# One head, both token tiles: how the differential attention of a hybrid trunk is cut into pieces

## The chip, the cores and the metric

The kernel runs on one core of a Trainium2 chip. The metric is the device time of one execution in microseconds (us). The engines of the core are named as in the profile: PE (TensorE, matmuls; PEld its weight loads), DVE (VectorE), ACT (ScalarE), POOL (GpSimd) and SP (SyncE, which issues most of the transfers). Each engine takes its instructions in order; semaphores make one wait for another. PE writes to PSUM banks, in which a row holds 512 fp32 values.

## The reference

Two layers on 256 tokens of width 2048, all in fp32, each with attention and a short gated convolution side by side and then an MLP. Cut to what the change touches:

```python
q = _rmsnorm(q.reshape(B, S, N_HEADS, 2, HEAD_DK), q_norm_g[l])     # 8 heads, 2 maps of 64
k = _rmsnorm(k.reshape(B, S, N_HEADS, 2, HEAD_DK), k_norm_g[l])
v = v.reshape(B, S, N_HEADS, HEAD_DV)                               # 128 wide
...
s = jnp.einsum('bqhmd,bkhmd->bhmqk', qb, k).astype(jnp.float32) * scale + bias
s = jnp.where(dist >= 0, s, NEG)
p = jax.nn.softmax(s, axis=-1)
p = p[:, :, 0] - lam * p[:, :, 1]
return jnp.einsum('bhqk,bkhd->bqhd', p.astype(v.dtype), v)
...
attn = (_rmsnorm(attn, subln_g[l]) * (1.0 - lam_init)).reshape(B, S, ATTN_WIDTH)
conv = gate_b * _short_conv(gate_c * conv_in, conv_w[l])
x = x + jnp.concatenate([attn, conv.astype(attn.dtype)], axis=-1) @ w_out[l]
hm = _rmsnorm(x, mlp_norm_g[l]) @ w_up[l]
x = x + jnp.square(jax.nn.relu(hm)) @ w_down[l]
```

Each head has two maps (m = 0, 1) of 64 columns. Their softmaxes are subtracted with a weight, the difference is multiplied with the head's values, and the result is normalised per head.

## The kernel before

The 256 tokens are two tiles of 128 (t = 0, 1). Every fp32 product is made of three fp32r products: an operand is split into a high part (rounded, made on ACT) and a low part (the rest, made on DVE), and high·high, high·low and low·high are summed in PSUM (`TERMS`). Weights are streamed from memory and split in the same way, one job of 128x1024 at a time: ACT makes `whi` (L282), DVE `wlo` (L283). Three buffers hold these jobs, so the conversion of a job three ahead can begin when PE has finished a job.

A layer is `mixer` and then `mlp`. `mixer` goes through the heads in two halves of four: the projections q, k and v of a half (`linear`, L338), then the convolution's gc and ci and later gb (`linear_t`, L360), then the output projection o (L338). PE's order is the program's order; the other engines' order is set by the scheduler when the kernel is built. Everything small is a generator that is advanced between the products of a projection: `Background` keeps the pieces, and each `tick` (after six products 512 wide in `linear`, and four times per job of eight products 512 wide and eight 256 wide in `linear_t`) advances those whose time has come; `yield n` puts a piece off by n ticks. `staggered` starts several pieces some ticks apart.

- `qk_norm` (L452 to L484), started when a q or k projection is done: squares (L461), reduction, factors and the scaled tile (L469), eight ticks of rest, four transposes per token tile into one bank (L478), from which ACT makes the high part (L481) and DVE the low part (L482). In the result, `qT` or `kT`, head i has map 0 in rows 0 to 63 and map 1 in rows 64 to 127.
- `attention` (L486 to L567), started three ticks after a v projection. Half 0's runs beside the q, k and v projections of half 1; half 1's beside gc and ci. It has eight units, (t, i) for a token tile and a head, started four ticks apart. A unit makes, for each map, three products on 64 rows into a bank (L500; 128 keys wide for t = 0 and 256 for t = 1), adds the bias and takes the maximum in one DVE instruction that empties the bank (L503), then the exponentials on ACT (L510), reciprocal, factors and the combined p on DVE (L513 to L521). Nine ticks later it transposes p (L526) and splits it (L528, L529), and four ticks later multiplies it with v (L536): three products 128 wide per key tile, into a quarter of one bank (tag `av`, one buffer) that the four heads of a token tile share. After the fourth head the bank is emptied (L544), squared (L549), the factors go through POOL (L551, L382, L554), the tile is scaled (L556), and nine ticks later transposed (L562) and split into `cat` (L565, L566), which the output projection reads.

PSUM has four banks for the projections' two accumulators, three for everything named `bank` (scores, transposes) and one for `av`. The pool `bpool` holds eight tiles for qT, kT, v, the bias's raw form, `cat` and `cv`.

Of the kernel before, what the change touches and what calls it, by code (L numbers as in the profile page):

```python
# [9 lines left out]
F32 = mybir.dt.float32  # L10
# [5 lines left out]
P = 128  # L16
DEPTH = 2
# [84 lines left out]
def trunk(ctx: ExitStack, tc: tile.TileContext, x, w_in, w_out, conv_w, q_norm_g, k_norm_g,  # L102
# [8 lines left out]
    nat = ctx.enter_context(tc.tile_pool(name="nat", bufs=7))  # L111
# [29 lines left out]
    ngv = const.tile([NG, P], F32, tag="ngv", name="ngv")  # L141
# [23 lines left out]
    vec = const.tile([ROWS, P], F32, tag="vec", name="vec")  # L165
    nc.gpsimd.dma_start(vec[0:NCW, :], conv_w.rearrange("l i (k p) -> (l i k) p", p=P))
    for i, g in enumerate((q_norm_g, k_norm_g)):
        for m in range(2):
            nc.gpsimd.dma_start(
                vec[QG + i * DEPTH:QG + (i + 1) * DEPTH, m * DK:(m + 1) * DK], g)  # L170
    nc.gpsimd.dma_start(vec[QG + 2 * DEPTH:MG, :], subln_g)
    nc.gpsimd.dma_start(vec[MG:ROWS, :], mlp_norm_g.rearrange("l (k p) -> (l k) p", p=P))
    lamv = const.tile([1, 4, DEPTH, DK], F32, tag="lamv", name="lamv")
    for i, a in enumerate((lambda_q1, lambda_q2, lambda_k1, lambda_k2)):
        nc.gpsimd.dma_start(lamv[:, i], a[None])
    sel = const.tile([NB + 1, REL], F32, tag="sel", name="sel")
    nc.gpsimd.dma_start(sel, selector)
    rel = const.tile([NB + 1, 2 * NH], F32, tag="rel", name="rel")
    nc.vector.memset(rel[NB:NB + 1, :], NEG)
    nc.gpsimd.dma_start(rel[0:NB, :], rel_bias)  # L180
# [15 lines left out]
    def small_setup():  # L196
# [3 lines left out]
        by_dist = const.tile([2 * NH, REL], F32, tag="bydist", name="by_dist")  # L200
# [12 lines left out]
        prod = const.tile([1, 2, DEPTH, DK], F32, tag="lprod", name="lprod")  # L213
# [13 lines left out]
    def load_bias(l, bpool, bias):  # L227

        if l == 0:
            yield from small_setup()  # L230
# [224 lines left out]
    def qk_norm(acc, r, dst, gain, name):  # L455
# [18 lines left out]
        yield 8  # L474
        for t in range(NT):
            tp = bank(f"{name}tp{t}")
            for i in range(4):
                nc.tensor.transpose(tp[:, i * P:(i + 1) * P], out_[t][:, i * P:(i + 1) * P], ident)  # L478
            tp3 = tp.rearrange("p (h c) -> p h c", c=P)
            hi, lo = (dst[:, i, :, t * P:(t + 1) * P] for i in range(2))  # L480
            nc.scalar.activation(hi, tp3, AF.Copy, scale=gain)  # L481
            nc.vector.scalar_tensor_tensor(lo, tp3, gain, hi.bitcast(F32),  # L482
                                           op0=ALU.mult, op1=ALU.subtract)
            yield 1  # L484

    def attention(l, qT, kT, v, h0, dst, bias, tmp):  # L486

        parts = dst.open()
        avs, r0s = {}, {}

        def unit(t, i):
            W = (t + 1) * P
            h = h0 + i
            s = tmp.tile([P, 2, S], F32, tag="s", name=f"s{h}_{t}")
            mx = small.tile([P, 2], F32, tag="mx", name=f"mx{h}_{t}")
            su = small.tile([P, 2], F32, tag="su", name=f"su{h}_{t}")
            for m in range(2):
                sc = bank(f"sc{h}_{t}_{m}")
                for n, (a, b) in enumerate(TERMS):
                    nc.tensor.matmul(  # L500
                        sc[:, :W], qT[m * DK:(m + 1) * DK, a, i, t * P:(t + 1) * P],
                        kT[m * DK:(m + 1) * DK, b, i, :W], start=(n == 0), stop=(n == 2))
                nc.vector.tensor_tensor_reduce(  # L503
                    out=s[:, m, :W], in0=sc[:, :W], in1=bias[:, 2 * h + m, S - W:],
                    op0=ALU.add, op1=ALU.max, scale=1.0, scalar=-3.0e38,
                    accum_out=mx[:, m:m + 1])
            nm = small.tile([P, 2], F32, tag="nm", name=f"nm{h}_{t}")
            nc.vector.tensor_scalar_mul(nm, mx, -1.0)
            for m in range(2):
                nc.scalar.activation(s[:, m, :W], s[:, m, :W], AF.Exp, bias=nm[:, m:m + 1],  # L510
                                     accum_out=su[:, m:m + 1])
            rc = small.tile([P, 2], F32, tag="rc", name=f"rc{h}_{t}")
            nc.vector.reciprocal(rc, su)  # L513
            if i == 0:
                r0s[t] = small.tile([P, 4], F32, tag="r0", name=f"r0_{h0}_{t}")
            nc.vector.tensor_copy(r0s[t][:, i:i + 1], rc[:, 0:1])
            c = small.tile([P, 1], F32, tag="c", name=f"c{h}_{t}")
            nc.vector.scalar_tensor_tensor(c, su[:, 0:1], rc[:, 1:2], nlam[:, l:l + 1],
                                           op0=ALU.mult, op1=ALU.mult)
            p = tmp.tile([P, S], F32, tag="p", name=f"p{h}_{t}", bufs=2)  # L520
            nc.vector.scalar_tensor_tensor(p[:, :W], s[:, 1, :W], c, s[:, 0, :W],  # L521
                                           op0=ALU.mult, op1=ALU.add)
            yield 9
            tp = bank(f"ptp{h}_{t}")
            for b in range(t + 1):
                nc.tensor.transpose(tp[:, b * P:(b + 1) * P], p[:, b * P:(b + 1) * P], ident)  # L526
# [500 lines left out]
```

## Time and profile before

| | |
|---|---|
| time, median of 3 runs | 2181.18 us (2179.99 to 2181.38) |
| the profiled execution: its own time, its span | 2181.14 us, 2179.4 us |
| granted TensorE clock | 0.999 |
| busy: PE, DVE, ACT, POOL | 2156.6, 1603.9, 1271.7, 138.8 us |
| weight split L282 on ACT, L283 on DVE | 386 each, 406.8 and 473.3 us |

The span is the profiled execution from its first to its last instruction; the time is a little longer than it. Busy times of groups on PE add up to more than the engine's, since matmuls overlap; what a product costs is read from start to start. In a row of groups stand the line, the engine, the operation, output and input, shapes and count, then busy time in us and the mean of one in ns, then the idle time before it with the instruction that ended it.

### The profile page before, as it was taken

What the parts mean: (1) busy time and instruction counts of PE and PEld (TensorE: products, weight loads), DVE (VectorE), ACT (ScalarE), POOL (GpSimd) and SP (SyncE); (2) the same over time, 40 slices, a digit from 0 to 9 for tenths busy, and PEclk for the clock granted to TensorE, in tenths of its full rate; (3) what the DMA queues carried; (4) which work ended last, traced back from release to release, by engine and by line L of the source; (5) the groups of instructions that cost most, each with busy time, mean ns of one, the idle gap of its engine ahead of it and who ended that gap; (6) DMA issues with size and microseconds to landing.
All of it is one profiled execution on the core that took longest, in us unless ns stands there. A gap on an engine that the chain in (4) does not pass through costs nothing.

```text
span 2179.4 us, 29050 instructions
## 1 busy us (share of the span) xinstructions
PE 2156.6 (99%) x11066; PEld 1828.6 (84%) x11066; DVE 1603.9 (74%) x2229; ACT 1271.7 (58%) x1718; POOL 138.8 (6%) x194
## 2 busy tenths in 40 slices
PE   8999999999999999999999999999999999999999
PEld 6888888888888888888888888888888888888887
DVE  6677655698888888855566776557988888887554
ACT  6456445566666666654454654455666666665443
POOL 2021100000000000100011111000000000001000
PEclk9999999999999999999999999999999999999999
DMA  7555656476666666587565466656766666666774
GB/s 256 180 156 177 218 185 184 157 238 223 213 212 215 220 208 214 189 277 241 175 205 181 156 199 197 184 173 190 225 218 217 213 212 216 219 208 212 246 242 145
DMA packets 292491, 446.62 MB, mean 205 GB/s; under 512 B 10403, under 2 KB 191221, under 8 KB 292352
## 3 DMA queue, kind: packets, MB, share of 16 engines
q1 hardware_dynamic: 285648, 423.66, 61.5%
q0 software_dynamic: 6656, 21.10, 2.6%
q8 instruction: 86, 1.41, 0.3%
q14 instruction: 53, 0.43, 0.1%
q10 hardware_dynamic: 48, 0.02, 0.0%
HBM read 425.84 MB, written 18.90 MB: 204 GB/s over the span
## 4 chain that ended last, share of the span: by engine, by line
PE 94%; DMA 2%; DVE 2%; ACT 1%; issue 1%; SPq 0%; DVEq 0%; ACTq 0%
PE upc L809 29%; PE dn L969 15%; PE pr L849 13%; PE o L338 8%; PE q L338 4%; PE gc L360 4%; PE ci L360 4%; PE k L338 4%; PE gb L360 4%; PE v L338 4%; PE upw L809 1%; DMA uraw<-in_w_up_dram 1%; PE sc L500 1%; PE av L536 1%; PE tpn L402 1%; DMA draw<-in_w_down_dram 1%
## 5 line engine op out<-in xcount | busy, mean ns | idle before, releaser
L283 DVE TENSOR_TENSOR wlo<-raw,whi 128x1024 fp32r<-128x1024 f32 (+1 forms) x386 | 473.3, 1228 | 385.5 <-ACT whi L282 381.0
L282 ACT ACTIVATE whi<-raw 128x1024 fp32r<-128x1024 f32 (+1 forms) x386 | 406.8, 1055 | 477.8 <-PE dn L969 166.7
L809 PE MATMUL upc<-nT,uhi 128*128 128x512 f32 x1920 | 477.5, 391 | 0.0
L694 ACT ACTIVATE uhi<-uraw 128x1024 fp32r<-128x1024 f32 x256 | 271.2, 1060 | 287.3 <-PE upc L809 253.9
L809 PEld LDWEIGHTS upc<-nT,uhi 128*128 128x128 f32 x1920 | 352.7, 188 | 68.2
L695 DVE TENSOR_TENSOR ulo<-uraw,uhi 128x1024 fp32r<-128x1024 f32 x256 | 312.8, 1222 | 115.3 <-ACT uhi L694 112.9
L969 PE MATMUL dn<-whi,g 128*128 128x512 f32 x1024 | 316.4, 389 | 0.0
L809 PEld LDWEIGHTS upc<-nT,ulo 128*128 128x128 f32 x1920 | 261.9, 190 | 18.7
L809 PE MATMUL upc<-nT,ulo 128*128 128x256 f32 x1920 | 267.7, 282 | 0.0
L969 PEld LDWEIGHTS dn<-whi,g 128*128 128x128 f32 x1024 | 192.2, 188 | 39.7
L969 PE MATMUL dn<-wlo,g 128*128 128x512 f32 x512 | 199.6, 390 | 1.1 <-DVE wlo L283 1.0
L338 PE MATMUL o<-whi,cat 128*128 128x512 f32 x512 | 159.6, 390 | 0.0
L969 PEld LDWEIGHTS dn<-wlo,g 128*128 128x128 f32 x512 | 96.1, 188 | 22.6 <-DVE wlo L283 2.8
L338 PEld LDWEIGHTS o<-whi,cat 128*128 128x128 f32 x512 | 96.2, 188 | 19.7
L338 PE MATMUL o<-wlo,cat 128*128 128x512 f32 x256 | 99.6, 389 | 0.0
L831 POOL DMA_DIRECT2D hid<-h x64 | 34.9, 545 | 949.1 <-ACT h L830 913.4
L849 PE MATMUL pr<-t13h,f 128*128 128x512 f32 x240 | 93.8, 391 | 0.0
L338 PE MATMUL q<-whi,nT 128*128 128x512 f32 x256 | 86.4, 406 | 4.1 <-ACT nT L248 4.1
L338 PE MATMUL k<-whi,nT 128*128 128x512 f32 x256 | 85.3, 399 | 0.0
L849 PE MATMUL pr<-t24h,f 128*128 128x512 f32 x240 | 84.0, 391 | 0.0
L849 PE MATMUL pr<-b2h,f 128*128 128x512 f32 x240 | 84.0, 391 | 0.0
L338 PE MATMUL v<-whi,nT 128*128 128x512 f32 x256 | 83.4, 396 | 0.0
(330 smaller groups left out, 3431.0 us busy)
## 6 DMA issues: line engine op xcount, KB each, us to landing
uraw<-in_w_up_dram SPq DMA_DIRECT2D x128, 1024.0 KB, 5.9
raw<-in_w_in_dram SPq DMA_DIRECT2D x192, 512.0 KB, 3.9
draw<-in_w_down_dram SPq DMA_DIRECT2D x64, 1024.0 KB, 5.1
raw<-in_w_down_dram SPq DMA_DIRECT2D x64, 1024.0 KB, 5.7
raw<-in_w_out_dram SPq DMA_DIRECT2D x64, 512.0 KB, 3.6
hid<-h POOLq DMA_DIRECT2D x64, 256.0 KB, 4.3
back<-hid SPq DMA_DIRECT2D x32, 512.0 KB, 3.3
rev<-by_dist_d POOLq DMA_DIRECT2D x4, 1024.0 KB, 11.1
```

Of the source, the lines that this page charges most:

```text
L282: nc.scalar.activation(hi[:, k], raw[:, k], AF.Copy)
L283: nc.vector.tensor_sub(lo[:, k], raw[:, k], hi[:, k].bitcast(F32))
L338: nc.tensor.matmul(acc[:, t], a.ap[:, pa, k % KG, t * P:(t + 1) * P], (hi, lo)[pw][:, j], start=(k == 0 and n == 0), stop=(k == nk - 1 and ...
L360: nc.tensor.matmul(acc[:, f, 0] if part else acc[:, f], wt[:, k % 4, fs], a.ap[:, 0, k % KG] if part else a.ap[:, :, k % KG], start=(part ...
L402: nc.tensor.transpose(tp[:, i * S + t * P:i * S + (t + 1) * P], xs[n][:, t, k * P:(k + 1) * P], ident)
L500: nc.tensor.matmul(sc[:, :W], qT[m * DK:(m + 1) * DK, a, i, t * P:(t + 1) * P], kT[m * DK:(m + 1) * DK, b, i, :W], start=(n == 0), stop=(n ...
L694: nc.scalar.activation(hi, src, AF.Copy)
L695: nc.vector.tensor_sub(lo, src, hi.bitcast(F32))
L809: nc.tensor.matmul(acc[:, 0] if part else acc, wt[:, k], a.ap[:, 0, k % KG] if part else a.ap[:, :, k % KG], start=(part == 0 and kh == 0 ...
L831: nc.gpsimd.dma_start(hid[i // 2][:, i % 2 * 2 * S:(i % 2 + 1) * 2 * S], u)
L849: nc.tensor.matmul(prods[n], fs[j][:, pa, a], b[pw], start=(j == 0 and m == 0), stop=(stop and m == 2))
L969: nc.tensor.matmul(acc[:, t], f[:, pa, k, t * P:(t + 1) * P], (hi, lo)[pw][:, k % 2], start=(b == 0 and k == 0 and m == 0), stop=(b == NB2 ...
```

## The change

A unit is now a head with both token tiles, and four units start eight ticks apart.

- Scores. `q_parts` puts the high part of map m in its own 64 rows and the low part in the other 64, in a block of its own per map; `k_parts` puts the high part of k in both halves of the rows, and a second tile `kL` holds k's low part in one half and zeros in the other (filled once per layer on POOL). A product on all 128 rows with the first gives high·high and low·high at once, and one with `kL` gives high·low. So a head has eight products instead of twelve: two per map and token tile. The two banks of a head (one per map) each hold both token tiles, and the products alternate between them.
- Each ACT and DVE step of q's and k's parts works on 64 partitions, so there are twice as many, and k's high part is written once more. `qk_norm` rests ten ticks instead of eight.
- Softmax. The same steps for both token tiles in a row, with maximum, reciprocal and copy once per head; p is written over the first map's exponentials. The rest before the transposes is ten ticks instead of nine; three transposes go to one bank and are split in one step each on ACT and DVE.
- Values. Each head takes the bank `av` for itself: per key tile one product 256 wide with v's high and low part side by side and one 128 wide with the low part of p. The two sums are added when the bank is emptied: ACT copies the one (`low`), DVE adds the other into `ao`. The squares for the norm are taken head by head.
- The tail of the norm runs once per half for both token tiles, with eight factors at once, and the rest before its transposes is twelve ticks instead of nine.
- Room: `nat` has six buffers instead of seven, `tmp` fewer and larger tiles, and the small tiles of the setup lie in one tile of `bpool`, with their loads issued in `mixer`.

The diff, without the lines that leave the old attention (they are in the listing above):

```diff
-    nat = ctx.enter_context(tc.tile_pool(name="nat", bufs=7))
+    nat = ctx.enter_context(tc.tile_pool(name="nat", bufs=6))
...
-    ngv = const.tile([NG, P], F32, tag="ngv", name="ngv")
+    ngv = wide("ngv")[:NG, :P]
...
-    def small_setup():
+    def setup_loads(tile):
...
+        def part(rows, n):
+            at[0] += n
+            return tile[0:rows, at[0] - n:at[0]]
+
+        vec = part(ROWS, P)
+        nc.gpsimd.dma_start(vec[0:NCW, :], conv_w.rearrange("l i (k p) -> (l i k) p", p=P))
...
+    def small_setup(vec, lamv, sel, rel, prod, by_dist):
...
-    def qk_norm(acc, r, dst, gain, name):
+    HALF = (slice(0, DK), slice(DK, P))
+    def q_parts(dst):
+        def put(tp3, gain, c):
+            for m, r in enumerate(HALF):
+                hi, lo = dst[r, m, :, c], dst[HALF[1 - m], m, :, c]
+                nc.scalar.activation(hi, tp3[r], AF.Copy, scale=gain[r])
+                nc.vector.scalar_tensor_tensor(lo, tp3[r], gain[r], hi.bitcast(F32),
+                                               op0=ALU.mult, op1=ALU.subtract)
+        return put
+    def k_parts(dst, low):
+        def put(tp3, gain, c):
+            for m, r in enumerate(HALF):
+                hi, lo = dst[r, m, :, c], low[r, m, :, c]
+                nc.scalar.activation(hi, tp3[r], AF.Copy, scale=gain[r])
+                nc.vector.scalar_tensor_tensor(lo, tp3[r], gain[r], hi.bitcast(F32),
+                                               op0=ALU.mult, op1=ALU.subtract)
+                nc.scalar.activation(dst[HALF[1 - m], m, :, c], tp3[r], AF.Copy, scale=gain[r])
+        return put
+    def qk_norm(acc, r, put, gain, name):
                 acc[:, t].rearrange("p (g d) -> p g d", d=DK),
                 f2.unsqueeze(2).to_broadcast([P, NH, DK]), op=ALU.mult)
             out_.append(qn)
...
+        yield 10
         for t in range(NT):
             tp = bank(f"{name}tp{t}")
             for i in range(4):
                 nc.tensor.transpose(tp[:, i * P:(i + 1) * P], out_[t][:, i * P:(i + 1) * P], ident)
...
+            put(tp.rearrange("p (h c) -> p h c", c=P), gain, slice(t * P, (t + 1) * P))
             yield 1
...
+    def attention(l, qT, kT, kL, v, h0, dst, bias, tmp):
         parts = dst.open()
...
+        OFF = (0, P)
+        r0 = small.tile([P, 4, NT], F32, tag="r0", name=f"r0_{h0}", bufs=2)
+        ss = small.tile([P, 4, NT], F32, tag="ams", name=f"ams{h0}", bufs=2)
+        ao = tmp.tile([P, NT, CH], F32, tag="ao", name=f"ao{h0}", bufs=1)
+        def unit(i):
             h = h0 + i
...
+            s = tmp.tile([P, 2, 3 * P], F32, tag="s", name=f"s{h}", bufs=2)
+            mx = small.tile([P, NT, 2], F32, tag="mx", name=f"mx{h}")
+            su = small.tile([P, NT, 2], F32, tag="su", name=f"su{h}")
+            sc = [bank(f"sc{h}_{m}") for m in range(2)]
+            for flip in range(2):
+                for k in (kT, kL):
+                    for t in range(NT):
+                        W, m = (t + 1) * P, t ^ flip
+                        nc.tensor.matmul(
+                            sc[m][:, OFF[t]:OFF[t] + W], qT[:, m, i, t * P:(t + 1) * P],
+                            k[:, m, i, :W], start=(k is kT), stop=(k is kL))
+            for t in range(NT):
+                W = (t + 1) * P
+                for m in range(2):
+                    nc.vector.tensor_tensor_reduce(
+                        out=s[:, m, OFF[t]:OFF[t] + W], in0=sc[m][:, OFF[t]:OFF[t] + W],
+                        in1=bias[:, 2 * h + m, S - W:], op0=ALU.add, op1=ALU.max, scale=1.0,
+                        scalar=-3.0e38, accum_out=mx[:, t, m:m + 1])
+            nm = small.tile([P, NT, 2], F32, tag="nm", name=f"nm{h}")
             nc.vector.tensor_scalar_mul(nm, mx, -1.0)
...
+            for t in range(NT):
+                for m in range(2):
+                    e = s[:, m, OFF[t]:OFF[t] + (t + 1) * P]
+                    nc.scalar.activation(e, e, AF.Exp, bias=nm[:, t, m:m + 1],
+                                         accum_out=su[:, t, m:m + 1])
+            rc = small.tile([P, NT, 2], F32, tag="rc", name=f"rc{h}")
             nc.vector.reciprocal(rc, su)
...
+            nc.vector.tensor_copy(r0[:, i], rc[:, :, 0])
+            c = small.tile([P, NT], F32, tag="c", name=f"c{h}")
+            p = s[:, 0]
+            for t in range(NT):
+                w = slice(OFF[t], OFF[t] + (t + 1) * P)
+                nc.vector.scalar_tensor_tensor(c[:, t:t + 1], su[:, t, 0:1], rc[:, t, 1:2],
+                                               nlam[:, l:l + 1], op0=ALU.mult, op1=ALU.mult)
+                nc.vector.scalar_tensor_tensor(p[:, w], s[:, 1, w], c[:, t:t + 1], s[:, 0, w],
+                                               op0=ALU.mult, op1=ALU.add)
+            yield 10
+            tp = bank(f"ptp{h}")
+            for b in range(3):
                 nc.tensor.transpose(tp[:, b * P:(b + 1) * P], p[:, b * P:(b + 1) * P], ident)
...
+            pT = tmp.tile([P, 2, 3 * P], F32R, tag="pT", name=f"pT{h}", bufs=1)
+            nc.scalar.activation(pT[:, 0], tp[:, :3 * P], AF.Copy)
+            nc.vector.tensor_sub(pT[:, 1], tp[:, :3 * P], pT[:, 0].bitcast(F32))
             yield 4
...
+            av = ps.tile([P, CH], F32, tag="av", name=f"av{h}", bufs=1)
+            av = av.rearrange("p (t n c) -> p t n c", t=NT, n=2)
+            for t in range(NT):
+                for k in range(t + 1):
+                    w = slice(OFF[t] + k * P, OFF[t] + (k + 1) * P)
+                    nc.tensor.matmul(av[:, t], pT[:, 0, w], v[:, :, k, i * P:(i + 1) * P],
+                                     start=(k == 0), stop=False, skip_group_check=True)
+                    nc.tensor.matmul(av[:, t, 0], pT[:, 1, w], v[:, 0, k, i * P:(i + 1) * P],
+                                     start=False, stop=(k == t), skip_group_check=True)
+            low = nat.tile([P, NT, P], F32, tag="wide", name=f"avl{h}")
+            nc.scalar.activation(low, av[:, :, 1], AF.Copy)
+            mine = slice(i * P, (i + 1) * P)
+            nc.vector.tensor_add(ao[:, :, mine], av[:, :, 0], low)
+            for t in range(NT):
+                nc.scalar.activation(low[:, t], ao[:, t, mine], AF.Square,
+                                     accum_out=ss[:, i, t:t + 1])
             if i < 3:
                 return
...
+            flat = ss.rearrange("p i t -> p (i t)")
+            rflat = r0.rearrange("p i t -> p (i t)")
             for _ in range(2):
...
+                nc.gpsimd.tensor_tensor(flat, flat, rflat, op=ALU.mult)
+            f = rstd_of(flat, P, f"a{h0}", 4 * NT)
+            f2 = small.tile([P, 4, NT], F32, tag="af2", name=f"af2{h0}", bufs=2)
+            nc.gpsimd.tensor_tensor(f2.rearrange("p i t -> p (i t)"), f, rflat, op=ALU.mult)
+            an_ = []
+            for t in range(NT):
+                an = wide(f"an{h0}_{t}")
+                nc.vector.tensor_tensor(
+                    an.rearrange("p (g d) -> p g d", d=P),
+                    ao[:, t].rearrange("p (g d) -> p g d", d=P),
+                    f2[:, :, t:t + 1].to_broadcast([P, 4, P]), op=ALU.mult)
+                an_.append(an)
+            yield 12
+            for t in range(NT):
+                tp = bank(f"atp{h0}_{t}")
+                for b in range(4):
+                    nc.tensor.transpose(tp[:, b * P:(b + 1) * P], an_[t][:, b * P:(b + 1) * P],
+                                        ident)
+                tp3 = tp.rearrange("p (h c) -> p h c", c=P)
+                hi = parts[:, 0, :, t * P:(t + 1) * P]
+                nc.scalar.activation(hi, tp3, AF.Copy, scale=s_gain[:, l:l + 1])
+                nc.vector.scalar_tensor_tensor(
+                    parts[:, 1, :, t * P:(t + 1) * P], tp3, s_gain[:, l:l + 1], hi.bitcast(F32),
+                    op0=ALU.mult, op1=ALU.subtract)
+                yield 2
+        yield from staggered([unit(i) for i in range(4)], 8)
         dst.ready = True
     def conv(l, q, u, cv, norm):
...
-            work.start(load_bias(l, bpool, bias), 10)
+            work.start(load_bias(l, bpool, bias, setup), 10)
+            kL = biasp.tile([P, 2, 4, S], F32R, tag="kL", name=f"kL{l}")
+            for m, r in enumerate(HALF):
+                nc.gpsimd.memset(kL[HALF[1 - m], m].bitcast(F32), 0.0)
-                work.start(qk_norm(acc, r, qT, q_gain[:, l:l + 1], f"q{l}{half}"))
+                work.start(qk_norm(acc, r, q_parts(qT), q_gain[:, l:l + 1], f"q{l}{half}"))
-                work.start(qk_norm(acc, r, kT, k_gain[:, l:l + 1], f"k{l}{half}"))
+                work.start(qk_norm(acc, r, k_parts(kT, kL), k_gain[:, l:l + 1], f"k{l}{half}"))
```

123 lines of the change are left out of this document (23 added, 100 removed).

## The prediction

> **What bounds the kernel now.** I read the page first, then the waits of PE, then PE's timeline beside the attention, then the groups of the vector and scalar engines.
>
> ```profile
> PE 2156.6 (99%) x11066; PEld 1828.6 (84%) x11066; DVE 1603.9 (74%) x2229; ACT 1271.7 (58%) x1718; POOL 138.8 (6%) x194
> ...
> PE 94%; DMA 2%; DVE 2%; ACT 1%; issue 1%; SPq 0%; DVEq 0%; ACTq 0%
> ```
>
> PE is busy 99% of the span and makes 94% of the chain that ended last. So a product saved is time saved, and any new wait of PE is time lost. Where PE waits today:
>
> ```profile
> PE q L338 <- ACT nT L248: 4.1, 1, 4.1
> PE gps L152 <- POOL ident masks.py:199: 3.5, 1, 3.5
> PE up L809 <- ACT ev L819: 3.2, 2, 2.0
> PE pr L849 <- DVE f L841: 3.2, 4, 1.0
> PE pr L935 <- DVE wlo L283: 1.6, 2, 0.8
> PE rbc L436 <- DVE diag L433: 1.1, 2, 0.5
> PE dn L969 <- DVE wlo L283: 1.0, 2, 0.6
> ```
>
> That is the whole list: start and MLP. No line of the attention is in it (scores L500, transposes L478 and L526, values L536): today the attention costs exactly the PE time of its products. Their price is read from the timeline (start, duration, line, tiles, shape, count), start to start, since matmuls overlap:
>
> ```profile
> 165.65 0.63 PE L360 MATMUL gc<-nT,wlo 128*128 128x256 f32 x4
> 166.21 0.56 PE L500 MATMUL sc<-kT,qT 64*128 64x128 f32 x6
> ...
> 167.27 1.09 PE L360 MATMUL gc<-nT,whi 128*128 128x512 f32 x4
> ...
> 188.45 0.63 PE L360 MATMUL ci<-nT,wlo 128*128 128x256 f32 x4
> 189.01 0.63 PE L500 MATMUL sc<-kT,qT 64*128 64x256 f32 x6
> ...
> 190.15 0.45 PE L536 MATMUL av<-v,pT 128*128 128x128 f32 x3
> ...
> 194.23 0.79 PE L536 MATMUL av<-v,pT 128*128 128x128 f32 x6
> 194.85 0.41 PE L526 MATMUL ptp<-ident,p 128*128 128x128 f32 x2
> 195.01 2.09 PE L360 MATMUL gc<-nT,whi 128*128 128x512 f32 x8
> 196.95 1.11 PE L360 MATMUL gc<-nT,wlo 128*128 128x256 f32 x8
> ...
> 205.72 0.78 PE L536 MATMUL av<-v,pT 128*128 128x128 f32 x6
> 206.34 2.04 PE L360 MATMUL gc<-nT,whi 128*128 128x512 f32 x8
> 208.22 1.11 PE L360 MATMUL gc<-nT,wlo 128*128 128x256 f32 x8
> 209.17 2.00 PE L360 MATMUL ci<-nT,whi 128*128 128x512 f32 x8
> 211.01 1.12 PE L360 MATMUL ci<-nT,wlo 128*128 128x256 f32 x8
> ```
>
> Undisturbed, eight products 256 wide take 209.17−208.22 = 0.95 us (0.12 each) and eight 512 wide 211.01−209.17 = 1.84 (0.23 each). A group put into such a run costs what it adds. Scores of token tile 0, put between twice four 256-wide products: 167.27−165.65−0.95 = 0.67. Scores of tile 1: 190.15−188.45−0.95 = 0.75. Six value products: 208.22−205.72−1.84 = 0.66, 0.11 each. Six and two transposes: 196.95−194.23−1.84 = 0.88, so a transpose is 0.11.
>
> **The change part by part.**
>
> Scores. Before, a head costs 0.67 + 0.75 = 1.42. After: eight products on all rows, four 256 wide and four 128 wide: 4 × 0.12 + 4 × 0.11 = 0.92. Gain 0.50 a head, 8.0 us over 16 heads (8 in each of 2 layers). The one unknown is whether the group keeps something of the old group's cost beyond its products. In the trace six products on 64 rows at 128 wide cost 0.67, six full-row ones 0.66, and two maps side by side should have halved that: by three pairs of 0.11 and 0.12, about 0.34 and 0.39 of a group is switching, together 0.7 a head. Full-row value groups, which also stand between projections, show no such edge, so I take none; kept in full once per new group (0.36) it would leave a gain of 2.2 us. These are the bounds: 2.2 to 8.0.
>
> The Trainium skill ("TensorEngine Tiling (Array Packing)", Overview and Key Properties) says that a contraction of at most 64 rows can be run as two row tiles, up to twice as fast, and that changing the tiling mode drains the engine. By the first sentence alone the old scores would be 3 × 0.11 + 3 × 0.12 = 0.69 a head and the change a loss of 0.23 a head, 3.7 us in all; the measured 1.42 decides against it and fits the drain.
>
> Values and their transposes. Nine products of 128 wide become three of 256 and three of 128: 9 × 0.11 − (3 × 0.12 + 3 × 0.11) = 0.30 a head, 4.8 us. Three transposes stay. All in all 12.8 us less PE work.
>
> q and k parts. Groups of the scalar engine (count, busy and mean ns, idle before):
>
> ```profile
> L282 ACT ACTIVATE whi<-raw 128x1024 fp32r<-128x1024 f32 x382 | 404.5, 1060 | 472.0 <-PE dn L969 166.7 <-PE o L338 73.6 <-PE v L338 39.1
> ...
> L510 ACT ACTIVATE s<-s,nm 128x128 f32<-128x128 f32 x32 | 12.5, 393 | 13.8 <-DVE nm L508 13.8
> ...
> L481 ACT ACTIVATE kT<-k01tp,gains 128x512 fp32r<-128x512 f32 x2 | 1.4, 690 | 1.1 <-PE k01tp L478 1.1
> ...
> L461 ACT ACTIVATE q01sq<-q,rowf 128x512 f32<-128x512 f32 x2 | 1.3, 668 | 0.0
> ```
>
> Twice as many scalar and vector operations per token tile, on half the partitions each, plus a copy for k's second half; how long a half-partition one takes no row shows, so I take the full one's 0.69 (the same number of columns; the other end, half of it, only eases this). All PE sees is when the last part lands, and qk_norm's wait grows from 8 ticks to 10. Per k, eight scalar operations of 0.69 and up to four conversions of 1.06 make 9.8 us; from k's second transposes to the first scores PE has eight ticks of six products, 8 × 6 × 0.23 = 11.0. So nothing; were two conversions more ahead, 0.9 per k, 3.6 in all. The zeros of kL are two fills per layer on POOL (6% busy) long before kL is read: nothing. The setup loads change their tile and keep their place at the head of POOL's queue, and the waits at the start (first two rows of the list) are for other things: nothing, or if they came late up to the few us that PE waits there now. The softmax is the same elements in fewer instructions; the norm tail on POOL goes from twice four columns to once eight, 12 ticks (some 8 us) ahead of its reader: nothing.
>
> New waits. The values now go through one bank ("av", one buffer) for every head, where four heads shared a bank before. Head i+1's first value product must wait until the scalar copy and the vector add have emptied head i's bank. In half 1 (beside gc and ci) the add stands well ahead. In half 0 (beside the q and k projections of half 1) the built order of the vector engine puts head 0's add behind head 2's softmax, two weight conversions and a q normalisation. The vector and scalar engines' timelines of before (182.86 to 185.72, start and duration) and the vector groups:
>
> ```profile
> 182.86 1.22 DVE L283 TENSOR_TENSOR wlo<-raw,whi 128x1024 fp32r<-128x1024 f32 x1
> 184.00 0.16 DVE L508 TENSOR_SCALAR nm<-mx 128x2 f32<-128x2 f32 x1
> ...
> 185.31 0.17 DVE L513 RECIPROCAL rc<-su 128x2 f32<-128x2 f32 x1 [0.97 <-ACT s L510]
> ...
> 185.72 0.42 DVE L503 CUSTOM_DVE_ANT_0 s<-sc,bias 128x256 f32<-128x256 f32 x1
> ```
>
> ```profile
> 184.19 0.51 ACT L510 ACTIVATE s<-s,nm 128x256 f32<-128x256 f32 x1 [1.02 <-DVE nm L508]
> ...
> 184.70 0.49 ACT L510 ACTIVATE s<-s,nm 128x256 f32<-128x256 f32 x1
> ```
>
> ```profile
> L503 DVE CUSTOM_DVE_ANT_0 s<-sc,bias 128x128 f32<-128x128 f32 x32 | 8.2, 286 | 2.9 <-PE sc L500 2.9
> ...
> L521 DVE SCALAR_TENSOR_TENSOR p<-s,c 128x256 f32<-128x256 f32 x16 | 7.7, 480 | 0.1
> L529 DVE TENSOR_TENSOR pT<-ptp,pT 128x256 fp32r<-128x256 f32 x16 | 6.7, 418 | 0.2
> ...
> L469 DVE TENSOR_TENSOR q01n<-q,q01f 128x512 f32<-128x512 f32 x2 | 1.4, 692 | 0.0
> ```
>
> Followed from the PE product that frees a weight buffer: a conversion on the scalar engine (1.06), the squares of q (0.67), four exponentials at 0.51 and, by their shorter length, some 0.40 (1.8), then on the vector engine reciprocal and factors (0.41 from 185.31 to 185.72 and one factor more: 0.5), the 384-wide pT (estimate 0.5, from 0.42 at 256), two p (0.48 and about 0.35), a conversion (1.14 start to start), q01n with its factor (0.7), a conversion (1.14) and the add (0.42). That is 8.8; with the overlaps of neighbours taken off on the scalar side and the hand-overs between engines put on, 9.1. PE has 30 products of 0.23 and three transposes until then, 7.3. So PE stands 1.8 us. Then the second q transposes of half 1 follow directly on head 3's scores and need one of the three banks; the one they get is that of head 3's second map, free when its two reductions are done (about 0.28 and 0.35, each with a short read): 0.9 us more after the previous wait. Together 2.7 us per layer, 5.4 us in all. Bounds: zero, if the add comes 1.8 us earlier than I string it together, and 10.0, if one conversion more stands ahead of each of the four waits (4 × 1.14 = 4.6 more).
>
> Sum: 2181.14 − 12.8 + 5.4 = 2173.7. The profiled 2181.14 stands 0.04 under the median of the runs, 2181.18, so nothing is shifted.
>
> **The rivals.**
>
> No new wait (2168.4): scalar and vector engines keep pace, 2181.14 − 12.8. For it: both have idle time (ACT 58%). Against: the sums above, and queues that run in order.
>
> The edges remain (about 2179.5): every score group, full rows or not, pays 0.36, so scores give 2.2 and not 8.0: 2181.14 − 2.2 − 4.8 + 5.4. For it: its bank changes from product to product, unlike any group seen. Against: the value groups at 0.11 a product.
>
> Slower, p late (about 2186): a head's softmax is now one long chain for both tiles: four reductions 1.6, four exponentials 1.8, factors 0.5, p 0.8, hand-overs about 0.6, and one conversion on each engine between, 7.5 us in all. From the scores to its transposes PE has ten ticks, in half 1 of 0.70 each (2.79 us for the eight and eight products from 209.17), with the neighbour's scores and values (0.92, 0.69) 8.6 us. Slack 1.1. One conversion pair more in front (1.06 + 1.14) makes every head 1.1 us late: 16 × 1.1 = 17.6, so 2181.14 − 12.8 + 17.6 = 2186. It decides once a head stands more than 0.8 us (12.8/16) late. Against it: the built order holds one pair in most heads, not two.
>
> **How the numbers follow.** Times within 0.2% of before (4.4 us, so 2176.8 to 2185.5) can't be told from no change. Chances: the forecast, 2170.5 to 2176.8, 0.52; no new wait 0.15; the edges, or first-half waits and k parts at their upper ends, 0.20, of which 0.03 still fall under 2176.8; p late 0.13. The predicted time is the likeliest one's, 2173.7. The range 2167.5 to 2184.0 takes in the first three but for a few in a hundred, and leaves out p late. Faster 0.52 + 0.15 + 0.03 = 0.70; same 0.17; slower 0.13.
>
> **What would show it.** PE's busy time down by about 12.8 us; a score group start to start near 0.92, and 0.69 for the values. In PE's waits two new rows, the value products behind the vector add (two times, near 1.8) and q01tp behind a score reduction (two times, near 0.9), nothing in half 1 and nothing at ptp. Wrong would be: score groups over 1.2; a row for ptp with eight or sixteen waits; a wait at the first scores of a half behind k's parts; or a start that moved.

## The result: slower, by a cost outside the attention

The changed kernel takes 2188.47 us (median of 6 runs, 2187.1 to 2190.34) against 2180.59 before (2179.09 to 2181.88): ratio 1.0037, interval [1.0024, 1.005]. Forecast were 2173.7 and the range 2167.5 to 2184.0. It is slower by 7.9 us where a gain of 7.4 was forecast.

The time is that of the slower rival (2186), but not its mechanism. That is seen in the list of PE's waits, after:

```profile
PE gps L152 <- POOL ident masks.py:199: 3.5, 1, 3.5
PE q L347 <- ACT nT L257: 3.4, 1, 3.4
PE av L578 <- DVE ao L585: 3.3, 2, 1.7
PE pr L905 <- DVE f L897: 2.9, 4, 1.0
PE up L865 <- ACT ev L875: 1.6, 2, 0.9
PE q11tp L513 <- DVE mx L542: 1.1, 1, 1.1
PE q01tp L513 <- DVE mx L542: 1.1, 1, 1.1
PE rbc L445 <- DVE diag L442: 1.1, 2, 0.5
PE pr L991 <- DVE wlo L292: 1.0, 2, 0.5
PE dn L1025 <- DVE wlo L292: 0.9, 2, 0.5
PE atp L610 <- DVE an L601: 0.4, 1, 0.4
```

The two new waits stand there as forecast: the values behind the vector add (twice, 1.7 us; forecast 1.8) and the q transposes behind a score reduction (1.1 each; forecast 0.9). No head waits for p. The prices of the groups in PE's timeline, after, beside the k and v projections of half 1:

```profile
111.49 0.39 PE L536 MATMUL sc<-kT,qT 128*128 128x128 f32 x2
111.72 0.40 PE L536 MATMUL sc<-kL,qT 128*128 128x128 f32 x2
111.95 0.39 PE L536 MATMUL sc<-kT,qT 128*128 128x128 f32 x2
112.18 0.40 PE L536 MATMUL sc<-kL,qT 128*128 128x128 f32 x2
112.42 0.39 PE L347 MATMUL k<-whi,nT 128*128 128x512 f32 x1
...
122.79 0.36 PE L578 MATMUL av<-v,pT 128*128 128x256 f32 x1 [1.66 <-DVE ao L585]
...
128.99 0.66 PE L513 MATMUL q01tp<-ident,q01n 128*128 128x128 f32 x4 [1.13 <-DVE mx L542]
...
138.02 0.28 PE L578 MATMUL av<-v,pT 128*128 128x256 f32 x1
...
138.66 0.45 PE L347 MATMUL v<-whi,nT 128*128 128x512 f32 x1
```

A score group takes 112.42 − 111.49 = 0.93 (forecast 0.92); a row names only its first product's shape. A value group takes 0.64 to the next product's start and, with what it adds to the product after it, 0.70 over 16 groups (forecast 0.69). So the attention did what was forecast. Yet PE's busy time rose:

```profile
PE 2162.2 (99%) x10954; PEld 1823.0 (83%) x10954; DVE 1610.7 (74%) x2197; ACT 1293.5 (59%) x1742; POOL 134.8 (6%) x178
```

112 products fewer than before, and 5.6 us more busy. Where it went shows in a table of stages, from the first product of each to the first of the next in PE's records, the last ending with PE's last product (us, both layers added):

| stage | before | after | difference |
|---|---|---|---|
| up to the end of half 0's first q | 35.8 | 33.7 | −2.1 |
| half 1's q, k, v and gc, ci (the attention runs beside these) | 361.5 | 355.6 | −5.9 |
| output projection o | 179.6 | 184.5 | +4.9 |
| MLP | 1390.3 | 1401.7 | +11.4 |
| all others | 203.4 | 203.4 | 0 |

The attention stretch gained 5.9 (forecast 12.8 − 5.4 = 7.4). The 16 us that turn it into a loss lie in o and in the MLP, whose code is the same; 9.9 of the MLP's 11.4 are in its down projection dn. There the products are a little slower. The groups of PE, before and then after:

```profile
L969 PE MATMUL dn<-whi,g 128*128 128x512 f32 x1024 | 316.4, 389 | 0.0
L969 PE MATMUL dn<-wlo,g 128*128 128x512 f32 x512 | 199.6, 390 | 1.1 <-DVE wlo L283 1.0
L338 PE MATMUL o<-whi,cat 128*128 128x512 f32 x512 | 159.6, 390 | 0.0
L338 PE MATMUL o<-wlo,cat 128*128 128x512 f32 x256 | 99.6, 389 | 0.0
```

```profile
L1025 PE MATMUL dn<-whi,g 128*128 128x512 f32 x1024 | 322.6, 395 | 0.0
L1025 PE MATMUL dn<-wlo,g 128*128 128x512 f32 x512 | 202.5, 396 | 1.0 <-DVE wlo L292 0.9
L347 PE MATMUL o<-whi,cat 128*128 128x512 f32 x512 | 162.7, 396 | 0.0
L347 PE MATMUL o<-wlo,cat 128*128 128x512 f32 x256 | 101.2, 395 | 0.0
```

6 ns more in each mean, in 2304 products. In the timelines, before and then after, three such products step 0.68 and 0.70 us:

```profile
1039.92 0.61 PE L969 MATMUL dn<-whi,g 128*128 128x512 f32 x2
...
1040.60 0.61 PE L969 MATMUL dn<-whi,g 128*128 128x512 f32 x2
...
1042.64 0.61 PE L969 MATMUL dn<-whi,g 128*128 128x512 f32 x2
```

```profile
1039.88 0.63 PE L1025 MATMUL dn<-whi,g 128*128 128x512 f32 x2
...
1040.58 0.63 PE L1025 MATMUL dn<-whi,g 128*128 128x512 f32 x2
...
1042.68 0.63 PE L1025 MATMUL dn<-whi,g 128*128 128x512 f32 x2
```

Twelve products take 1042.64 − 1039.92 = 2.72 us before and 1042.68 − 1039.88 = 2.80 after. Over all intervals without a wait the mean step of dn is 226.8 ns before and 233.3 after, of o 226.9 and 233.3. 2304 × 6.4 ns = 14.8 us. There is no wait, no lower clock, and the weight loads last as long (188 ns in either): the products themselves go slower, steadily, from the first to the last.

### The profile page after: what moved, and what is told of

Its sections match the earlier page's. It is cut to its first block, busy times and chain, and to the rows that moved or that the text cites. A ratio compares the mean times of both kernels' runs of the same rounds, so it can differ in the third digit from the quotient of the medians.

```text
span 2187.4 us, 28821 instructions
## 1 busy us (share of the span) xinstructions
PE 2162.2 (99%) x10954; PEld 1823.0 (83%) x10954; DVE 1610.7 (74%) x2197; ACT 1293.5 (59%) x1742; POOL 134.8 (6%) x178
## 4 chain that ended last, share of the span: by engine, by line
PE 93%; DVE 3%; DMA 2%; ACT 1%; issue 1%; SPq 0%; DVEq 0%; ACTq 0%
PE upc L865 29%; PE dn L1025 16%; PE pr L905 13%; PE o L347 8%; PE q L347 4%; PE gc L369 4%; PE gb L369 4%; PE ci L369 4%; PE v L347 4%; PE k L347 3%; PE upw L865 1%; DMA uraw<-in_w_up_dram 1%; DMA back<-hid 1%; PE sc L536 1%; PE tpn L411 1%
## 5 line engine op out<-in xcount | busy, mean ns | idle before, releaser
L1025 PE MATMUL dn<-whi,g 128*128 128x512 f32 x1024 | 322.6, 395 | 0.0
L905 PE MATMUL pr<-t13h,f 128*128 128x512 f32 x240 | 94.1, 392 | 0.0
L905 PE MATMUL pr<-b2h,f 128*128 128x512 f32 x240 | 84.3, 392 | 0.0
L905 PE MATMUL pr<-t24h,f 128*128 128x512 f32 x240 | 84.3, 392 | 0.0
```

The source lines that it names most:

```text
L905: nc.tensor.matmul(prods[n], fs[j][:, pa, a], b[pw], start=(j == 0 and m == 0), stop=(stop and m == 2))
L1025: nc.tensor.matmul(acc[:, t], f[:, pa, k, t * P:(t + 1) * P], (hi, lo)[pw][:, k % 2], start=(b == 0 and k == 0 and m == 0), stop=(b == NB2 ...
```

## The experiments

What did change for o and dn is where their operands lie. The change makes pools smaller and larger (`nat`, `tmp`, the setup tiles), so the tiles behind them lie elsewhere. In the built kernels the first weight half stands at byte 74592 of a partition and g at 188256 before, at 67360 and 178784 after: 113664 and 111424 bytes apart, which is 0 and 64 modulo 256. The first theory was that of the place, the rival that something works beside them in the new order. Unused bytes between pools tell these apart: they move tiles, and every engine's instructions and their order stay as they are.

```diff
-    small = ctx.enter_context(tc.tile_pool(name="small", bufs=4))
+    small = ctx.enter_context(tc.tile_pool(name="small", bufs=4)); ctx.enter_context(tc.tile_pool(name="pad", bufs=1)).tile([P, 16], F32, tag="pad", name="pad")
```

This is the edit for 64 bytes; the others have another number of fp32 in it.

**64 bytes in the changed kernel.**

> The changed kernel with 64 unused bytes per partition put behind the small tiles: every engine's instructions and their order are the same, only the tiles allocated behind them (g, cat, f, raw, kT, qT ...) lie 64 bytes higher, the weight halves, x and nT stay. Theory A (where tiles lie): a 512-wide product steps 227 ns when its moving and its stationary operand lie a multiple of 128 bytes apart, and 233 ns when they lie 64 bytes off; in the changed kernel this hits the 1536 products of dn and the 768 of o. Then this run takes 2304 x 6.5 ns = 15 us off: 2188.5 - 15 = 2173.5, dn and o step 227 again. Theory B (something that works beside them, transfers or other engines, is slower for the new order): the order is untouched, so 2188.5 and 233 stay.

**64 bytes in the kernel before.**

> The kernel before with the same 64 bytes at the same place, nothing of the attention changed. Theory A: now its dn and o operands lie 64 bytes off: 2180.6 + 15 = 2195.6, dn and o step 233. Theory B: 2180.6, step 227.

**128 and 32 bytes in the changed kernel.**

> The changed kernel with 128 bytes there. Theory A: distances are what they are without it, modulo 128: 2188.5, step 233. Theory B: 2188.5 too. A third theory, that any other place of the tiles would do (A without the 128): something else than 2188.5, near 2174.

> The changed kernel with 32 bytes there: distances of dn and o are 32 bytes off modulo 64. Theory A gives no figure beforehand; if only whole multiples of 128 are fast 2188.5 or more with a step of 233 or above, if the middle counts in part something between, near 2181. Theory B: 2188.5.

Measured, with ratios to the kernel before: 64 bytes 2184.34 (1.0022 [1.0013, 1.0032]); the kernel before with 64 bytes 2197.54 (1.0080 [1.0065, 1.0095]); 128 bytes 2179.25 (0.9999 [0.9990, 1.0009]); 32 bytes 2192.05 (1.0056 [1.0041, 1.0071]). The second run alone settles that it is not the attention: the kernel before, not an instruction moved, loses 18 us when some of its tiles move by 64 bytes, and its o and dn step 233.3. Its rows:

```profile
L969 PE MATMUL dn<-whi,g 128*128 128x512 f32 x1024 | 323.0, 396 | 0.0
L338 PE MATMUL o<-whi,cat 128*128 128x512 f32 x512 | 162.8, 396 | 0.0
```

Theory B falls. But theory A's rule falls too: with 64 bytes the changed kernel has its operands a multiple of 128 apart and still steps 232.9, and 128 bytes, which should have done nothing, brought 228.9.

The five steps, ordered by distance, suggested another rule, which the next runs tested; it is theory C in their expectations. The edit for 64 bytes ahead of everything puts the same unused tile in front of `xpool`.

> The changed kernel with 192 unused bytes behind the small tiles, order untouched. Theory C (distance): what counts is the distance between the weight halves (moving, ahead of the pad) and g or cat (stationary, behind it), taken modulo 1024 bytes: 0 in the kernel before (step 226.8 ns), and -192, -160, -128, -64 in the changed one without and with 32, 64 and 128 bytes (233.3, 234.2, 232.9, 228.9), +64 in the kernel before with 64 bytes (233.3). With 192 bytes it is 0 again: dn and o step 226.8, 2188.5 - 2304 x 6.5 ns = 2173.5, less about 1 us for the products of the MLP that follow. Rival D (chance of a build, any shift throws the dice anew): any step between 227 and 234, 2173 to 2192.

> The changed kernel with 256 bytes there: distance +64, as in the kernel before with 64 bytes. Theory C: step 233.3 and 2188.5. Rival D: anything from 2173 to 2192.

> The changed kernel with 64 bytes ahead of x, nT and the weight halves, so that every large tile moves by 64 and no distance changes. Theory C: as without, step 233.3 and 2188.5. If the absolute place counts (theory E: residues of each tile by itself): another step, as the 64 bytes behind the small tiles gave another one.

Measured: 192 bytes 2170.64 (0.9957 [0.9942, 0.9972]), 256 bytes 2187.46 (1.0035 [1.0021, 1.0049]), 64 bytes ahead of all 2189.11 (1.0041 [1.0026, 1.0056]). All three came out as theory C said, and D and E fall. The groups with 192 bytes have their means of before back, in a kernel that is otherwise the changed one:

```profile
L1025 PE MATMUL dn<-whi,g 128*128 128x512 f32 x1024 | 316.4, 389 | 0.0
L347 PE MATMUL o<-whi,cat 128*128 128x512 f32 x512 | 159.5, 390 | 0.0
```

So without the cost outside, the kernel is 2180.01 − 2170.64 = 9.4 us faster than the one before, in that comparison.

**The other pairs.** Is it the distance within a product's pair, or the place of g and cat? 64 and 256 bytes between nT and the weight halves (the same unused tile in front of `wpool`) move the weights against nT and leave them where they are against g and cat.

> The kernel before with 64 unused bytes between nT and the weight halves: everything from the weight halves on moves by 64, so the distances between weights and g, cat and f stay, and those between weights and nT become 64. Theory C says that it is the pair of a product that counts: dn and o stay at 226.8 ns, and the 512-wide products that have nT on one side (1152 of q, k and v, 768 of gc, ci and gb, 2048 of the MLP's up products) go to 233.3 from 228.3, 230.2 and 228.4: 5.8 + 2.4 + 10.0 = 18 us, 2198. If it were only the place of g and cat that counts: 2197 with dn and o slow and the others as they are, as in the run with 64 bytes behind the small tiles.

> The changed kernel with 256 bytes between nT and the weight halves: weights to g and cat stay at -192, so dn and o stay at 233.3; weights to nT come to 256. If the distance counts modulo 256 or less, 2188.5 and q, k, v and up as they are; if modulo 512 (the stationary slices within a tile lie 512 bytes apart and step alike, so it is not more), these are slower: up to 18 us, 2206.

Measured: 2178.52 (0.9994 [0.9985, 1.0004]) and 2188.24 (1.0038 [1.0025, 1.0051]). The steps of dn, o and the wide up products went as theory C said; those of q, k and v did only in part, and the time of the first run did not. The groups of the kernel before with the gap of 64:

```profile
L809 PE MATMUL upc<-nT,uhi 128*128 128x512 f32 x1920 | 486.1, 394 | 0.0
L969 PE MATMUL dn<-whi,g 128*128 128x512 f32 x1024 | 316.3, 389 | 0.0
L809 PE MATMUL upc<-nT,ulo 128*128 128x256 f32 x1920 | 258.6, 277 | 0.0
```

dn is untouched, so for it the pair counts, and not the place of g. One more rival moves with g in the runs before, since the unprocessed weights (`raw`) lie behind the small tiles too: the split reads raw and writes the weight halves, while PE multiplies. It doesn't fit. In gb the same split runs, its products have both operands ahead of the unused bytes, and they step 230.1 ns in the kernel before and in the changed one with 0, 32, 64, 128, 192 and 256 bytes alike. And with the gap of 64, which leaves raw and halves as far apart as they were, the up products do change. The 512-wide up products step 233.0 in place of 228.4, but the 256-wide ones between them became faster, 114.4 in place of 119.1, and give back just what the others lose. q, k and v, where the weights are the moving side and nT the stationary one, go from 228.3 to 229.5 only. My 18 us were wrong for both reasons: I took the effect as one number for every 512-wide product. The gap of 256 changed no step (up 229.6, q, k and v 228.3, as without it): distances count modulo 256, not 512.

The steps of dn then fall into one table, with the distance as address of the stationary minus that of the moving operand, modulo 256 bytes:

| distance | kernels | step of dn, ns |
|---|---|---|
| 0 | before; before with the gap; changed with 192 | 226.8 in all three |
| 64 | changed; changed with 256, with 64 ahead, with the gap; before with 64 | 233.3 in all five |
| 96 | changed with 32 | 234.3 |
| 128 | changed with 64 | 232.9 |
| 192 | changed with 128 | 228.9 |

The mild 1.2 ns of q, k and v with the gap fits in kind: their distance is −64, which is 192, where dn loses 2.1.

**The waits and the prices.** With the place put right, the two new waits were taken away by moving two rests, and on that kernel the prices of the two parts were tested one by one.

```diff
-            yield 4
+            yield 6
             av = ps.tile([P, CH], F32, tag="av", name=f"av{h}", bufs=1)
...
-        yield 10
+        yield 8
         for t in range(NT):
             tp = bank(f"{name}tp{t}")
```

> The changed kernel with 192 bytes as above, and its two new waits taken away by moving work: the rest between pT and the value products is six ticks instead of four, and qk_norm rests eight ticks as before the change instead of ten. Theory C with the prediction's price of the waits (2 x 1.7 for av, 2 x 1.1 for q01tp): 5.5 us less than the changed kernel with 192 bytes, about 2168, with no row of L578 or L513 in PE's waits. Rival: the waits come back elsewhere (scores waiting for k's parts, transposes for p), 2173.

Measured 2164.81 (0.9931 [0.9916, 0.9946]): 5.8 us less than with 192 bytes alone, forecast 5.5. That the two agree so closely is in part luck: in the profiled executions, which differ by 7.9 us, the attention stretch gives 4.9 (355.2 to 350.3), with 1.4 of new waits in it, and the MLP 2.5, which the forecast doesn't have. L578 is gone from PE's waits and the q transposes of half 1 (q01tp, q11tp) wait no more; of the attention these rows are left, the norm's tail and once the first q transposes of half 0 (a row of L513, which the expectation had excluded):

```profile
PE atp L610 <- DVE an L601: 1.4, 2, 0.7
...
PE q00tp L513 <- DVE q00n L504: 0.7, 1, 0.7
```

This is the fastest kernel of the study, 15 us ahead of the one before.

Scores on 64 rows again, in one group per head:

```diff
-            for flip in range(2):
-                for k in (kT, kL):
-                    for t in range(NT):
-                        W, m = (t + 1) * P, t ^ flip
+            for t in range(NT):
+                W = (t + 1) * P
+                for m in range(2):
+                    for n, (r, k) in enumerate(((HALF[m], kT), (HALF[m], kL), (HALF[m], kL))):
...
-                            sc[m][:, OFF[t]:OFF[t] + W], qT[:, m, i, t * P:(t + 1) * P],
-                            k[:, m, i, :W], start=(k is kT), stop=(k is kL))
+                            sc[m][:, OFF[t]:OFF[t] + W], qT[r, m, i, t * P:(t + 1) * P],
+                            k[r, m, i, :W], start=(n == 0), stop=(n == 2))
```

> late_values_shift192 with the scores made of twelve products on 64 rows again, in the order of before (three per map and token tile; the third repeats high times low in place of low times high, so the scores lack low times high and count the other correction twice). By the prediction's prices of a head, 1.42 in place of 0.92: 16 x 0.50 = 8.0 us more than 2164.8, 2172.8. If full-row groups kept the edges: 2167.

Measured 2177.63 (0.9989 [0.9979, 0.9998]), 12.8 more than without, and not for the reason forecast. Its timeline, and the top of its waits:

```profile
168.75 0.62 PE L369 MATMUL gc<-nT,wlo 128*128 128x256 f32 x4
169.30 0.33 PE L536 MATMUL sc<-kT,qT 64*128 64x128 f32 x2
169.46 0.39 PE L536 MATMUL sc<-kL,qT 64*128 64x128 f32 x4
169.69 0.34 PE L536 MATMUL sc<-kT,qT 64*128 64x256 f32 x2
169.86 0.40 PE L536 MATMUL sc<-kL,qT 64*128 64x256 f32 x4
170.19 0.74 PE L369 MATMUL gc<-nT,wlo 128*128 128x256 f32 x4
170.77 1.09 PE L369 MATMUL gc<-nT,whi 128*128 128x512 f32 x4
```

```profile
PE atp L610 <- DVE an L601: 8.3, 2, 5.1
```

The group costs 170.77 − 168.75 − 0.95 = 1.07 (1.09 over the eight that stand alone), not 1.42. The prediction's own numbers would have given nearly that: 0.69 for twelve products on 64 rows and one switch of some 0.36 make 1.05. The expectation took 1.42, the price of two groups, for one. So of the 0.50 that a head gains, about a third (1.09 − 0.92 = 0.17) comes from full rows, and two thirds from having one group in place of two, with one change into the 64-row mode and back. The Trainium skill ("TensorEngine Tiling (Array Packing)", Key Properties) says that a change of the tiling mode drains the engine. This agrees, at 1.42 − 1.09 = 0.33 us for one way in and back. By this estimate the twelve products alone take 1.09 − 0.33 = 0.76 us, less than the 0.92 of the eight on full rows; by it, full rows win only because they need no change of mode.

Scores then cost 0.17 more in the eight groups that stand alone and 0.11 more in the eight that follow a value group, 2.2 us in all, and the wait for the norm's tail grew from 1.4 to 8.3; why, was not looked into. The next part is the clock. PE's timeline around the longer of these two waits:

```profile
212.41 1.11 PE L610 MATMUL atp<-ident,an 128*128 128x128 f32 x4 [5.06 <-DVE an L601]
213.18 1.20 PE L369 MATMUL ci<-nT,wlo 128*128 128x256 f32 x4
214.18 1.05 PE L369 MATMUL ci<-nT,whi 128*128 128x512 f32 x2
```

Four 256-wide products take 214.18 − 213.18 = 1.00 us here, where eight took 0.95 undisturbed. The granted clock is 0.51 from 211.6 to 218.5 us and 1.0 on either side. The ci projection around it is 7.1 us longer than without the edit, of which the wait is 4.3; the slow products are the other 2.8. The 3.3 us wait at the same place in layer 1 leaves the clock at 1.0, so what lowers it isn't settled. Together these are 2.2 + 6.9 + 2.8 = 11.9 of the 12.8; the rest isn't settled.

Value products in two 128-wide ones:

```diff
-                    nc.tensor.matmul(av[:, t], pT[:, 0, w], v[:, :, k, i * P:(i + 1) * P],
+                    nc.tensor.matmul(av[:, t, 0], pT[:, 0, w], v[:, 0, k, i * P:(i + 1) * P],
                                      start=(k == 0), stop=False, skip_group_check=True)
+                    nc.tensor.matmul(av[:, t, 1], pT[:, 0, w], v[:, 1, k, i * P:(i + 1) * P],
+                                     start=(k == 0), stop=(k == t), skip_group_check=True)
```

> late_values_shift192 with each 256-wide value product made of two 128 wide (v's high and low part one after the other): nine products a head again, 0.11 each. By the prediction's prices 3 x (2 x 0.11 - 0.12) = 0.30 a head, 4.8 us: 2169.6; up to 1.4 more if the scores of head 5 wait for a bank. Rival: 256-wide products cost as much as two of 128, 2164.8.

Its values aren't the reference's. The two sums now begin one after the other in one bank and may disturb each other, which was not tested; number and size of all operations are as the edit says. Measured 2176.11 (0.9980 [0.9971, 0.9990]), 11.3 more. The price was right: eight steps of value products take 140.94 − 140.10 = 0.84 us in its timeline, 0.105 each,

```profile
140.10 0.22 PE L578 MATMUL av<-v,pT 128*128 128x128 f32 x1
...
140.94 0.28 PE L582 MATMUL av<-v,pT 128*128 128x128 f32 x1
```

and the group costs 1.01 over 16 in place of 0.70, 5.0 us in all. The rest is waits again:

```profile
PE atp L612 <- DVE an L603: 3.7, 2, 2.0
...
PE sc L536 <- DVE cat L617: 1.3, 2, 0.7
```

2.3 more for the norm's tail than in the kernel that it was made from, and the 1.3 for a bank that the expectation named. The clock falls here too: it is 0.50 from 212.8 to 216.2 us, behind the 2.0 us wait of layer 0, and the ci projection there is 1.6 longer than by its wait. The profiled execution is 12.8 us longer than that of the kernel that it was made from (2177.39 and 2164.55); with 2.5 in the first q stage and the MLP, which have no cause named, all but 0.1 of it is found.

## Why the prediction was wrong

The steps that it named held. Score group 0.92, measured 0.92 to 0.93. Values 0.69, measured 0.69 to 0.70. Transposes 0.33, measured 0.34. No edge on full-row groups: held. Value wait 1.8 a layer, measured 1.7. Wait of the second q transposes 0.9, measured 1.1. Nothing at p's transposes, nothing for k's parts: no row for either. Sum of the attention −7.4: measured −5.9 in its stretch, where one layer also waits 0.4 for the norm's tail, which was costed at nothing; the other 1.1 was not traced to a step.

The step that failed is in the sum itself, "2181.14 − 12.8 + 5.4 = 2173.7": it took every product that the change doesn't touch at the price of before. The one sentence on moved tiles, that the setup loads "change their tile and keep their place at the head of POOL's queue", asks only when they arrive; the sizes of the pools, and with them the places of all other tiles, were given no term and no reason for it. But the pools moved g, cat and f against the weights by 64 bytes modulo 256, and the 2304 products of o and dn went from 226.8 to 233.3 ns. That is 14.8 us by their count, and removing it alone turned 2188.5 into 2170.6, 17.8 us; the other 3 lie in the MLP's remaining products, which step 1 to 2 ns faster too (229.5 to 228.4 for the wide up products, 231.1 to 229.3 for the 512-wide ones of L905 and L991). That forecast and 14.8 add up to just 2188.5 is chance: a start that was 2.1 us shorter stands against an attention that gained 1.5 less and against 1.5 us more in the MLP outside dn. A start that moved was named as a sign of being wrong. It did move, but it does so without the change too: counted from PE's first product, the kernel before takes 35.8 us up to there, and 33.6 and 34.1 with 64 unused bytes at either place.

The page before held a hint. Undisturbed products of one shape had no single mean:

```profile
L360 PE MATMUL gb<-nT,whi 128*128 128x512 f32 x256 | 64.1, 392 | 0.0
```

That is 392 for gb against 389 for dn, both 128x512 and both without a wait. I read a product's step as a constant of its shape. The hint goes no further than that: gb's operands lie a multiple of 256 bytes apart as well, so its longer step has another cause, which was not looked for.

The slower rival gave nearly the right time, and by its sign a reader might take it as confirmed. It isn't: there is no row for p, and the run with 192 bytes has the same softmax chain and is 0.43% faster than before. Nor did the edges remain: full-row groups have none, and the prediction's reading of the old groups, some 0.36 of each for switching, fits the 0.33 that one group in place of two saves. What it leaves unsaid is where the credit belongs: most of the scores' gain is in putting the two token tiles together, not in the full rows.

Why the distance counts was not found. Whether the distance to a product's own stationary operand or to the next one's matters can't be told here, as their slices lie multiples of 256 bytes apart. Nor is the distance within a pair the whole rule. The products of the up projection and of L905, whose distances are 0 in all kernels without a gap, still step between some 225 and 237 ns, and their means move with the unused bytes: the wide up products 228.4 with 192, 229.5 with none, 230.4 with 32 or 128. The rule is shown for dn and o, and for products with nT by the one gap; what else acts in the MLP the runs don't explain.

## What to carry to other kernels

When a change alters the size of any pool, compare the means of the groups that it doesn't touch, since a shift of other tiles can outweigh what was done; here 64 bytes cost 0.8%. Where long runs of 512-wide products lead, look at the tile addresses and try a few unused bytes between pools until stationary and moving operand lie a multiple of 256 bytes apart, and measure the time: where wide and narrow products alternated, the wide ones' loss was made up for by the narrow ones. And judge a change only with that put right: this one is a loss of 0.37% as it stands, a gain of 0.43% with 192 unused bytes, and of 0.69% with its two waits moved as well. Read the granted clock behind a wait of some us, too: here one cost 2.8 us more than its length.

## What was not expected of the hardware

- A 512-wide fp32r product steps 226.8, 233.3, 234.3, 232.9 or 228.9 ns with its operands 0, 64, 96, 128 or 192 bytes apart modulo 256, steadily over 1500 products, at a granted clock of 0.999 to 1.0.
- Where 512-wide and 256-wide products with nT alternate, 64 bytes slow the wide ones by 4.6 ns and speed the narrow ones up by 4.7 (1920 each), and the time stays the same (2178.52 against 2180.31, a ratio of 0.9994).
- Twelve products on 64 rows cost 1.09 us in one group and 1.42 in two.
- Around a wait of PE of 5.1 us the granted clock was 0.51 for 6.9 us, and around one of 2.0 us 0.50 for 3.4; a wait of 3.3 us left it at 1.0.
